# Four small edits to the loads and one to the layout at the head of a gated-linear-attention kernel

## The chip, the core and the metric

The kernel runs on one core of a Trainium2 chip. The metric is device microseconds from the start to the end of one execution. Times of several runs are compared by their median. Beside the timed runs there is one execution taken by the hardware profiler, from which all lines of the profile come.

## The reference

One residual layer with a gated linear attention mixer (GLA), then a squared-ReLU MLP, then a final RMSNorm, all in float32. There are 256 tokens, the model width is 2048, there are 4 heads with keys of 256 and values of 512, and chunks of 64 tokens. Cut to what matters:

```python
def _gla_mixer(h, w_in, w_gate_up, b_gate, o_norm, w_out):
    proj = h @ w_in                              # q, k, v, r, g_low (16 columns)
    log_a = log_sigmoid(g_low @ w_gate_up + b_gate) / 16.0
    cum = cumsum(log_a, within a chunk of 64);  total = cum at the chunk's end
    k_dec = k * exp(total - cum)
    # over the chunks: state = exp(total) * state + k_dec^T v;  o = (q / 16) @ state
    o = rmsnorm per head(o) * o_norm
    return (o * silu(r)) @ w_out

h = x + _gla_mixer(_rmsnorm(x, gla_norm), ...)
h = h + square(relu(_rmsnorm(h, mlp_norm) @ w_up)) @ w_down
out = _rmsnorm(h, final_norm)
```

## The kernel before

Each float32 matmul is made of three: an operand is split into a high part (`hi`, rounded to the matmul's own format, by ScalarE, L118) and the rest (`lo`, by VectorE, L131 or L165), and the products hi·hi, hi·lo and lo·hi are added up in PSUM. The weights come from memory once, in tiles of 128 rows (`raw`, six buffers), are split into `hi` and `lo` (five buffers each, of 1088 columns), and are used at once. `weights` does all this for one tile; SP's queue issues the loads, in order.

The work goes through stages. Only the first three matter here.

- **Stage 1** (`natural`, L176): 16 steps over `kt`, each with one tile of `w_vg` (the values' first 1024 columns and the 16 columns of the gate, 128 x 1040). A step is 24 matmuls: two halves of the tokens, three products, and the columns in four parts, of which three are 256 wide and one is 272. The stationary operand is the input, the moving one the weights. For the first two steps the tile is loaded and cast in pieces. The input itself, transposed (`xt`), is loaded in pieces of several `kt` each by `input_tile`, which is called while step `kt` is written; `x_loads` says at which step which piece is issued, and where it ends. `split_input` multiplies the input row by the norm's gain (`colt`, loaded from `cols`) and splits it (L326 on ScalarE, L327 on VectorE).
- **The key halves** (`turned`, L219): 8 pairs of `kt` for each of two halves of the key columns; a pair is one load of 2 x 128 rows by 512 columns and 24 matmuls, the first 12 with the pair's first 128 rows, the other 12 with its second. Here the weights are stationary and the input moves. The first half overlaps with the end of stage 1 and with the gate's own work (two transposes, L413, and eight matmuls, L422).
- **The query halves**, of the same form.

Behind these come the rest of the projections, the attention, the output projection (L715) and the MLP (L857), where GpSimd's queue issues loads that add into a tile in place (L734, L1067).

Small pieces of work are put between the steps by hand: `side` is a queue of functions, and `pump` calls one (or a few) after each step. `load_gate` in this queue issues the three loads of the gate's weights into `wgu`, and `split_gate` splits them into `wgs`. `tc.issue_after` orders an instruction behind another of the same engine; otherwise a scheduler with a cost model sets the order on each engine. [...]

Where operands lie within a tile is chosen by hand too. Input rows are 320 elements apart and are read by the key halves from element 64 on. A pair's weights lie from element 48 on, the second 128 rows directly behind the first, 512 elements further. With `gap` (the pairs listed in `even`), the second rows lie 16 elements further:

```python
between = SLOT - OFF - 2 * GT if gap else 0
to = [a[:, OFF - between : OFF + 2 * GT + between].rearrange("p (i c) -> p i c", i=2)[:, :, between:] for a in to]
```

so that they start at element 576, which, like 64, is a multiple of 32. The same is done at some later places of the kernel (`EVEN`, `BOTH`, `even` in `up`).

Of the kernel before, what the change touches and what calls it, by code (L numbers as in the profile page):

```python
# [36 lines left out]
KT = D // P  # L37
# [3 lines left out]
KEYW = HEADS * DK  # L41
RANK = 16
# [5 lines left out]
GT = 512  # L48
# [20 lines left out]
def tile_gla_mlp(ctx, tc, x, xt, cols, w_vg, w_in, w_gate, w_out, w_up, w_down, final_norm, out):  # L69
    nc = tc.nc  # L70
# [11 lines left out]
    def psum_bank(i, name="acc"):  # L82
        return psum.tile([P, 512], F32, tag=f"b{i}", name=name)

    def acc_banks(n):
        acc_free.rotate(-n)
        return [psum_bank(acc_free[k - n]) for k in range(n)]

    def aux_bank():
        aux_free.rotate(-1)  # L90
        return psum_bank(aux_free[-1], "aux")


    side = deque()

    def pump(n=1):

        with tc.issue_after(last_hi[0].ins), tc.issue_after(last_lo[0].ins):
            for _ in range(n):
                if side:  # L100
                    side.popleft()()
# [8 lines left out]
    last_load, last_hi, last_lo, last_sum, last_end = [None], [None], [None], [None], [None]  # L110

    def copy_hi(to, raw):
        with ExitStack() as order:
            if last_end[0]:
                order.enter_context(tc.issue_after(last_end[0]))
            if ordered[0]:
                order.enter_context(tc.issue_after(last_hi[0].ins))
            last_hi[0] = nc.scalar.copy(to, raw)  # L118

    def slots():  # L120
        return [wpool.tile([P, SLOT], F32R, tag=i, name=i) for i in ("hi", "lo")]

    def parts(raw, n, to, pieces=None):

        hi, lo = to
        for s in (slice(*p) for p in pieces or [(0, n)]):
            copy_hi(hi[:, s], raw[:, s])
            with ExitStack() as order:
                if last_sum[0]:
                    order.enter_context(tc.issue_after(last_sum[0]))  # L130
                last_lo[0] = nc.vector.tensor_tensor(lo[:, s], raw[:, s], hi[:, s].bitcast(F32), op=ALU.subtract)  # L131
        return hi, lo
# [3 lines left out]
    def raw_tile():  # L136

        if n_raw[0] is not None:
            n_raw[0] += 1
            if n_raw[0] % 7 == 0:  # L140
                return wpool.tile([P, G], F32, tag="more", name="raw", bufs=1)
        return wpool.tile([P, WMAX], F32, tag="raw", name="raw", bufs=6)

    def weights(src, n, pieces=None, room=None, gap=None):


        to = room or slots()
        raw = raw_tile()
        loads, pieces = pieces or ([(0, n)], [(0, n)])
        for s in (slice(*p) for p in loads):  # L150
            dst = raw[:, s]
            if len(src.shape) == 3:
                dst = dst.rearrange("p (i c) -> p i c", i=2)
                with ExitStack() as order:

                    if n_raw[0] == 7:
                        order.enter_context(tc.issue_after(last_load[0].ins))
                    last_load[0] = nc.sync.dma_start(out=dst, in_=src)
                between = SLOT - OFF - 2 * GT if gap else 0
                to = [a[:, OFF - between : OFF + 2 * GT + between].rearrange("p (i c) -> p i c", i=2)[:, :, between:] for a in to]  # L160
                copy_hi(to[0], dst)
                with ExitStack() as order:
                    if last_sum[0]:
                        order.enter_context(tc.issue_after(last_sum[0]))
                    last_lo[0] = nc.vector.tensor_tensor(to[1], dst, to[0].bitcast(F32), op=ALU.subtract)  # L165
                return to
            else:
                last_load[0] = nc.sync.dma_start(out=dst, in_=src[:, s])  # L168
        return parts(raw, n, to, pieces)

    def halves(o, x, w, first, last):
# [31 lines left out]
    def pair_of(w, kp, c0, even):  # L203
        return weights(w[2 * kp * P : 2 * (kp + 1) * P, c0 : c0 + GT].rearrange("(i p) c -> p i c", p=P), 2 * GT, gap=kp in even)

    def turned(row, w, c0, even=(0,), acc=None):

        acc = acc or acc_banks(GT // P // 2)
        for kp in range(KT // 2):
            wh, wl = pair_of(w, kp, c0, even)  # L210
            for i in range(2):
                kt = 2 * kp + i
                ah, al = row(kt)
                for j in range(GT // P):
                    s = slice(j * P, (j + 1) * P)
                    o = acc[j // 2][:, j % 2 * T : (j % 2 + 1) * T]
                    for n, (u, m) in enumerate(((wh, ah), (wh, al), (wl, ah))):

                        nc.tensor.matmul(  # L219
                            o, u[:, i, s], m, start=kt == 0 and n == 0 and j % 2 == 0,  # L220
                            stop=kt == KT - 1 and n == 2, skip_group_check=True,
                        )
                if kt < KT - 1:
                    pump()
        return acc
# [12 lines left out]


    colt = const.tile([P, 44], F32, name="colt")  # L240
    nc.scalar.dma_start(out=colt, in_=cols)
    g1 = lambda kt: colt[:, kt : kt + 1]
    g2 = lambda kt: colt[:, KT + kt : KT + kt + 1]
    go = lambda i: colt[:, 2 * KT + i : 2 * KT + i + 1]
# [28 lines left out]
    def x_row(kt, lo, hi):  # L273
        return [a[:, kt - CUT * (kt >= CUT), lo:hi] for a in xs[kt >= CUT]]

    stream_x = lambda kt: x_row(kt, WRAP, WRAP + T)
# [24 lines left out]
    xr = zz.rearrange("p a b t -> p (a b) t")  # L301
    cuts = [(0, 512), (512, 768), (768, WMAX)]
    x_done = [0]
    x_loads = {0: 1, 1: 3, 3: 6, 5: 9, 7: 12, 9: KT}

    def input_tile(kt):
        if kt in x_loads:
            s = slice(x_done[0], x_loads[kt])

            with ExitStack() as order:  # L310
                if kt >= 7:
                    order.enter_context(tc.issue_after(last_load[0].ins))
                nc.sync.dma_start(out=xr[:, s, :], in_=xv[:, s, :])
            x_done[0] = x_loads[kt]
        with ExitStack() as order:
            if kt >= FINE:
                order.enter_context(tc.issue_after(last_hi[0].ins))
                order.enter_context(tc.issue_after(last_lo[0].ins))
            split_input(kt)
        return ([(0, 512), (512, WMAX)], [(0, 256), (256, 512), (512, WMAX)]) if kt < 2 else None  # L320

    def split_input(kt):
        if kt == KT - 1:
            wrap_input(0, 0, CUT)
        h, l = x_row(kt, 0, T)
        nc.scalar.activation(h, xr[:, kt, :], AF.Copy, scale=g1(kt))  # L326
        nc.vector.scalar_tensor_tensor(l, xr[:, kt, :], g1(kt), h.bitcast(F32), op0=ALU.mult, op1=ALU.subtract)  # L327
        if kt in EVEN:
            i = EVEN.index(kt)
            nc.scalar.copy(xe[:, 0, i], h[:, :P].bitcast(F32))  # L330
            nc.vector.tensor_copy(xe[:, 1, i], l[:, :P].bitcast(F32))
# [3 lines left out]
    wgu = mid.tile([GR, KEYW], F32, tag="db", name="wgu")  # L335
# [8 lines left out]
    def load_h(t, half):  # L344
        c = slice(half * G, (half + 1) * G)
        with tc.issue_after(last_load[0].ins):
            nc.sync.dma_start(out=h[:, t, c], in_=x[t * P : (t + 1) * P, c])

    def load_gate():
        for p in (0, 32, 64):  # L350
            nc.scalar.dma_start(out=wgu[p : p + RANK, :], in_=w_gate)

    ms1 = st.tile([P, NT], F32, name="ms1")

# [17 lines left out]
        nc.vector.tensor_tensor(wgs[64:GR, :], wgu[64:GR, :], wgs[64:GR, :].bitcast(F32), op=ALU.subtract)  # L372

    nothing = lambda: None
    side.extend([clear_gate] + [nothing] * 4 + [load_gate] + [nothing] * 2 + [split_gate])
    side.extend([nothing, lambda: load_h(0, 0), lambda: load_h(0, 1), lambda: (load_h(1, 0), load_h(1, 1))])
    side.extend([lambda: token_ssq(0), lambda: (token_ssq(1), token_rsqrt())])


# [4 lines left out]
    def put_v(bank, n, t, c0):  # L384
# [4 lines left out]
        )  # L389

    acc = natural(plain_x, rows(w_vg, 0, WMAX), WMAX, cuts, ahead=input_tile)
    flush()
    wrap_input(1, 0, KT - CUT)
# [88 lines left out]
        nc.vector.tensor_tensor(kab[:, 0, c], kab[:, 0, c], zz[:, 1, c], op=ALU.mult)  # L482

    for half in range(2):
        acc = turned(stream_x, w_in, KEYW + half * GT, even=(0,) if half else (2, 3), acc=None if half else [aux_bank(), aux_bank()])
        for b in range(2):
            c0 = 4 * half + 2 * b
            from_bank(kab[:, 0, c0 : c0 + 2], acc[b])
# [15 lines left out]
    for half in range(2):  # L504
        acc = turned(stream_x, w_in, half * GT, even=())
# [41 lines left out]
    acc = natural(row_x, rows(w_in, 3 * KEYW), G, HALF, order=even_at(9, 11))  # L547
# [88 lines left out]
    acc = natural(lambda kt, t: (plain_x if kt == EVEN[1] else row_x)(kt, t), rows(w_in, 4 * KEYW), G, HALF, order=even_at(0, 6))  # L636
# [50 lines left out]
    acc = natural(row_x, rows(w_in, 5 * KEYW), G, HALF, order=even_at(2, 4))  # L687
# [322 lines left out]
    acc = [[], []]  # L1010
# [232 lines left out]
    for t in range(NT):  # L1243
# [19 lines left out]
        for on_act, lo, hi in ((0, 0, 256), (1, 1280, 1536), (0, 256, 768), (1, 1536, 2048), (0, 768, 1280)):  # L1263
            s = hf[:, t, lo:hi]
# [44 lines left out]
```

## Time and profile before

| | us |
|---|---|
| median of 3 runs | 1044.01 |
| lowest, highest | 1043.68, 1044.53 |
| the profiled execution, its time | 1044.42 |
| its span, from the first to the last instruction | 1042.4 |
| TensorE busy (matmuls) | 1034.2 |
| VectorE busy | 865.6 |
| ScalarE busy | 737.1 |
| GpSimd busy | 119.8 |

The granted TensorE clock was 0.998 of full speed over the span. Engines are named PE (TensorE matmul), PEld (its weight loads, which overlap), DVE (VectorE), ACT (ScalarE), POOL (GpSimd) and SP; a small q behind the name is the engine's queue, which issues loads. A row of the timeline gives the start, the duration, the engine, the line, the operation, output<-input, the shape, and in brackets the idle time of the engine ahead of it with what ended it. In groups of instructions x is the count, followed by busy time and the mean of one in ns. A row of the windows gives a stretch, its length, the busy time of an engine with its instructions, the granted clock, the share of DMA time and GB/s. In the chain of waits a row is start, duration, and what ran.

### The profile page before, as it was taken

Reading aid. Unit: us, or ns where it says so; the run is one execution under the profiler, and the core shown is the slowest. Engines: PE = TensorE matmul, PEld = TensorE weight load, DVE = VectorE, ACT = ScalarE, POOL = GpSimd, SP = SyncE. Lnnn points to the kernel's source line nnn. Section 1 sums busy time; section 2 is a strip of 40 time slices with the busy share of each in tenths; the row PEclk is TensorE's granted clock in tenths of the full one; section 3 lists DMA queues with packets and bytes.
Section 4 is the critical chain, followed back from the end, with each engine's and each line's share of the span. In section 5 each row is a group of like instructions: output and inputs, shape, how many; then the busy total and the mean of one; then the engine's idle time right before and its main releaser. Section 6 shows DMA issues by size and latency. Waiting matters only on the chain.

```text
span 1042.4 us, 23169 instructions
## 1 busy us (share of the span) xinstructions
PE 1034.2 (99%) x9058; PEld 1033.3 (99%) x9058; DVE 865.6 (83%) x1171; ACT 737.1 (71%) x1088; POOL 119.8 (11%) x163
## 2 busy tenths in 40 slices
PE   9999999999999999999999999999999999999997
PEld 9999999999999999999999999999999999999997
DVE  5768654656499876889999999999999999999887
ACT  6785544546477764677788788778778778878685
POOL 0000000010111101111111111111111111211100
PEclk9999999999999999999999999999999999999999
DMA  9957665555667786678887888887888888887772
GB/s 339 333 170 212 194 198 165 157 148 182 184 188 206 214 260 194 175 213 227 232 236 230 242 229 225 233 240 219 243 236 224 248 228 229 234 232 220 233 242 90
DMA packets 118733, 226.79 MB, mean 218 GB/s; under 512 B 10672, under 2 KB 27184, under 8 KB 118496
## 3 DMA queue, kind: packets, MB, share of 16 engines
q1 hardware_dynamic: 100096, 207.39, 63.3%
q0 software_dynamic: 17856, 16.26, 10.3%
q8 instruction: 71, 1.16, 0.4%
q10 hardware_dynamic: 672, 1.66, 0.4%
q14 instruction: 38, 0.31, 0.1%
HBM read 223.17 MB, written 2.10 MB: 216 GB/s over the span
## 4 chain that ended last, share of the span: by engine, by line
PE 96%; DMA 2%; issue 1%; ACT 0%; DVE 0%; SPq 0%; POOLq 0%; POOL 0%; DVEq 0%; ACTq 0%
PE up L857 33%; PE acc L857 28%; PE acc L176 17%; PE acc L715 8%; PE acc L219 6%; PE aux L219 2%; DMA raw<-in_w_vg 2%; PE aux L176 1%; PE aux L620 1%; PE aux L521 1%; DVE lo L131 0%; ACT hi L118 0%; ACT sqf L1196 0%; SPq L168 0%; PE acc L422 0%
## 5 line engine op out<-in xcount | busy, mean ns | idle before, releaser
L118 ACT CAST hi<-raw 128x512 fp32r<-128x512 f32 (+4 forms) x634 | 512.1, 834 | 231.5 <-PE acc L176 64.3
L131 DVE TENSOR_TENSOR lo<-raw,hi 128x768 fp32r<-128x768 f32 (+3 forms) x226 | 238.1, 1057 | 95.9 <-ACT hi L118 93.2
L857 PE MATMUL acc<-hi,act 128*128 128x256 f32 x1696 | 247.7, 276 | 0.0
L857 PE MATMUL up<-hh,hi 128*128 128x256 f32 x1024 | 238.7, 276 | 0.0
L857 PE MATMUL up<-hl,hi 128*128 128x256 f32 x1024 | 238.7, 276 | 0.0
L165 DVE TENSOR_TENSOR lo<-raw,hi 128x1024 fp32r<-128x1024 f32 x160 | 194.8, 1220 | 28.2 <-ACT hi L118 26.2
L857 PEld LDWEIGHTS acc<-hi,act 128*128 128x128 f32 x1696 | 217.6, 188 | 0.0
L857 PEld LDWEIGHTS up<-hh,hi 128*128 128x128 f32 x1024 | 192.3, 188 | 0.0
L857 PEld LDWEIGHTS up<-hl,hi 128*128 128x128 f32 x1024 | 192.3, 188 | 0.0
L1067 POOL DMA_DIRECT2D raw<-in_w_down x112 | 97.4, 869 | 516.9 <-DMA raw<-in_w_down 245.5
L1127 DVE TENSOR_TENSOR lo<-raw,hi 128x1024 fp32r<-128x1024 f32 x112 | 136.4, 1218 | 1.1 <-ACT hi L118 1.1
L857 PE MATMUL up<-hh,lo 128*128 128x256 f32 x1024 | 137.0, 276 | 0.0
L857 PE MATMUL acc<-lo,act 128*128 128x256 f32 x848 | 133.8, 276 | 0.0
L857 PEld LDWEIGHTS up<-hh,lo 128*128 128x128 f32 x1024 | 125.7, 188 | 0.0
L857 PEld LDWEIGHTS acc<-lo,act 128*128 128x128 f32 x848 | 113.3, 188 | 0.0
L176 PE MATMUL acc<-hi,xA 128*128 128x256 f32 (+1 forms) x728 | 105.2, 278 | 0.0
L176 PEld LDWEIGHTS acc<-hi,xA 128*128 128x128 f32 x728 | 93.5, 188 | 0.5 <-ACT hi L118 0.5
L598 DVE TENSOR_TENSOR raw<-raw 128x512 f32<-128x512 f32 x124 | 85.6, 691 | 3.2
L176 PE MATMUL acc<-lo,xA 128*128 128x256 f32 (+1 forms) x364 | 60.8, 278 | 0.1
L597 DVE TENSOR_TENSOR raw<-raw 128x256 f32<-128x256 f32 x124 | 52.4, 423 | 2.9
L176 PEld LDWEIGHTS acc<-lo,xA 128*128 128x128 f32 x364 | 50.3, 188 | 0.3 <-DVE lo L131 0.3
L219 PE MATMUL acc<-xA,hi 128*128 128x256 f32 x288 | 49.2, 276 | 0.0
(181 smaller groups left out, 1225.9 us busy)
## 6 DMA issues: line engine op xcount, KB each, us to landing
raw<-in_w_up SPq DMA_DIRECT2D x128, 512.0 KB, 4.5
raw<-in_w_down SPq DMA_DIRECT2D x224, 256.0 KB, 4.5
raw<-in_w_in SPq DMA_DIRECT2D x80, 512.0 KB, 3.7
raw<-in_w_down POOLq DMA_DIRECT2D x112, 128.0 KB, 5.2
raw<-in_w_out SPq DMA_DIRECT2D x20, 512.0 KB, 4.5
raw<-in_w_down SPq DMA_DIRECT2D x16, 512.0 KB, 4.9
raw<-in_w_vg SPq DMA_DIRECT2D x14, 520.0 KB, 8.4
raw<-in_w_out SPq DMA_DIRECT2D x24, 256.0 KB, 3.7
```

The source lines that it names most:

```text
L118: last_hi[0] = nc.scalar.copy(to, raw)
L131: last_lo[0] = nc.vector.tensor_tensor(lo[:, s], raw[:, s], hi[:, s].bitcast(F32), op=ALU.subtract)
L165: last_lo[0] = nc.vector.tensor_tensor(to[1], dst, to[0].bitcast(F32), op=ALU.subtract)
L176: nc.tensor.matmul(o[:, m], x, w[:, m], start=first and c == 0, stop=last, skip_group_check=True)
L219: nc.tensor.matmul(o, u[:, i, s], m, start=kt == 0 and n == 0 and j % 2 == 0, stop=kt == KT - 1 and n == 2, skip_group_check=True,)
L521: nc.tensor.matmul(o, kab[:, k[0], c0 + c, k[1] : k[1] + P], q(qt[:, c0 + c]), start=c == 0, stop=c == 1)
L597: nc.vector.tensor_tensor(u[:, 2], u[:, 0], u[:, 2], op=ALU.subtract)
L598: return nc.vector.tensor_tensor(u[:, 1::2], u[:, 1::2], u[:, 2:3].to_broadcast([P, 2, T]), op=ALU.subtract)
L715: newest[0] = nc.tensor.matmul(bank[:, o + d : o + d + T], x, w[:, d : d + T], start=bank in sums_banks and bank.name not in begun, stop=l ...
L857: newest[0] = nc.tensor.matmul(o, x, w, start=first, stop=last, skip_group_check=True).ins
L1067: nc.gpsimd.dma_start(out=raw[:, :T], in_=src[:, 0, T:], accum_op=ALU.add)
L1127: last_lo[0] = nc.vector.tensor_tensor(to[1][:, :G], u, to[0][:, :G].bitcast(F32), op=ALU.subtract)
```

## The change

- The three loads of the gate's weights are issued from GpSimd's queue and not from ScalarE's.
- The input comes in eight pieces and not in six; from the third on each ends earlier or is issued at a later step. The last two rows are issued at step 14 and no longer at step 9.
- The first piece of the first weight tile is issued from ScalarE's queue; the norms' columns, which ScalarE's queue had issued first, come from SP's queue, behind the first input piece.
- In the first key half, pair 0 joins pairs 2 and 3 in having its second rows 16 elements further.
- `split_gate` is called one step later in the side queue.

```diff
             else:
-                last_load[0] = nc.sync.dma_start(out=dst, in_=src[:, s])
+                queue = nc.sync if last_load[0] else nc.scalar
+                last_load[0] = queue.dma_start(out=dst, in_=src[:, s])
...
     colt = const.tile([P, 44], F32, name="colt")
-    nc.scalar.dma_start(out=colt, in_=cols)
...
-    x_loads = {0: 1, 1: 3, 3: 6, 5: 9, 7: 12, 9: KT}
+    x_loads = {0: 1, 1: 3, 3: 5, 5: 8, 8: 10, 10: 12, 12: 14, 14: KT}
...
                 nc.sync.dma_start(out=xr[:, s, :], in_=xv[:, s, :])
+            if kt == 0:
+                nc.sync.dma_start(out=colt, in_=cols)
...
         for p in (0, 32, 64):
-            nc.scalar.dma_start(out=wgu[p : p + RANK, :], in_=w_gate)
+            nc.gpsimd.dma_start(out=wgu[p : p + RANK, :], in_=w_gate)
...
-    side.extend([clear_gate] + [nothing] * 4 + [load_gate] + [nothing] * 2 + [split_gate])
-    side.extend([nothing, lambda: load_h(0, 0), lambda: load_h(0, 1), lambda: (load_h(1, 0), load_h(1, 1))])
+    side.extend([clear_gate] + [nothing] * 4 + [load_gate] + [nothing] * 3)
+    side.extend([split_gate, lambda: load_h(0, 0), lambda: load_h(0, 1), lambda: (load_h(1, 0), load_h(1, 1))])
...
     for half in range(2):
-        acc = turned(stream_x, w_in, KEYW + half * GT, even=(0,) if half else (2, 3), acc=None if half else [aux_bank(), aux_bank()])
+        acc = turned(stream_x, w_in, KEYW + half * GT, even=(0,) if half else (0, 2, 3), acc=None if half else [aux_bank(), aux_bank()])
```

In the order of instructions that follows, the identity and the zeroing on GpSimd are followed directly by the three gate loads. On ScalarE the two casts of the first weight piece now come ahead of the first input row, and on TensorE the first four matmuls are followed by four that need the second weight piece. The transposes of the gate stand after 59 and 62 matmuls of the first key half, where they stood after 67 and 70, and six of the gate's matmuls after 90, where they stood after 98. From the second key half on, TensorE's order is as before.

## The prediction

> **What bounds the kernel now.** I read the page first: how much of the span TensorE works.
>
> ```profile
> span 1042.4 us, 23169 instructions
> PE 1034.2 (99%) x9058; PEld 1033.3 (99%) x9058; DVE 865.6 (83%) x1171; ACT 737.1 (71%) x1088; POOL 119.8 (11%) x163
> ```
>
> TensorE is busy 1034.2 of 1042.4 us, so an edit can win only what TensorE waits, or what its matmuls take too long. Next, the view of who waited for whom, cut to TensorE's weight loads: after the warm-up these are all its waits in the whole span.
>
> ```profile
> PEld acc L176 <- ACT hi L118: 0.5, 2, 0.3
> PEld acc L176 <- DVE lo L131: 0.3, 1, 0.3
> ```
>
> All three belong to L176, and so to the first stage (16 steps over `w_vg`). Its steps begin where the timeline shows the first matmuls of a new `kt`; the view of busy time by stretches, one stretch per step (0, 1, 2, 3, 5, 6, 7; the first number after the stretch is its length), gives:
>
> ```profile
> 4.44:7.42 2.98, 2.98 (x25) 1.00 1.03 343
> 7.42:10.64 3.22, 3.22 (x27) 1.00 0.98 350
> 10.64:13.52 2.88, 2.88 (x27) 1.00 1.03 420
> 13.52:16.40 2.88, 2.88 (x27) 1.00 1.02 410
> 19.28:22.36 3.08, 3.04 (x26) 1.00 1.02 390
> 22.36:25.66 3.30, 3.25 (x24) 1.00 1.03 310
> 25.66:28.54 2.88, 2.88 (x26) 1.00 1.02 417
> ```
>
> An undisturbed step takes 2.88 us at a granted clock of 1.00. Steps 0 and 1 lose 0.10 and 0.34 us, steps 5 and 6 lose 0.20 and 0.42, the others shown nothing. So 0.44 us lies at the start and 0.62 us around 22 us. The second thing to be won is the spacing of matmuls of one and the same form (128x256). The chain of waits has long unbroken runs of them; the view of one line's instructions has their duration:
>
> ```profile
> 52.21 7.42 PE aux L219 x63
> 60.21 3.31 PE aux L219 x28
> 65.58 9.53 PE aux L219 x84
> L219 PE MATMUL aux<-xA,hi x32: 279/279/279, 52.8 to 58.3; 128*128 128x256 f32 x32
> L219 PE MATMUL acc<-xA,hi x7: 283/283/283, 76.4 to 77.5; 128*128 128x256 f32 x7
> L219 PE MATMUL acc<-xA,hi x271: 276/276/276, 77.9 to 134.6; 128*128 128x256 f32 x136
> ```
>
> 9.53 us / 84 is 113.5 ns a matmul; 7.42 / 63 is 117.8, and 3.31 / 28 is 118.2. So there is a quick pace (duration 276) and one 4.3 ns slower (279). The slow one holds from the first stage to about 63 us; the 283s at 76.4 to 77.5 are the second half of the pair that `even=(0,)` marks in the next half, and behind them the pace is quick. I read this as a lock: a disturbance throws TensorE into the slow pace, and a dozen matmuls whose weights lie at the same place as the input rows (weights at element 48+528=576, inputs at 64, both multiples of 32; an unmarked pair has its weights 16 off) put it back.
>
> **The change, part by part.**
>
> *Gate loads.* In the timeline, ScalarE's queue holds the three gate loads between two casts:
>
> ```profile
> 14.96 1.07 ACT L118 CAST hi<-raw 128x1040 fp32r<-128x1040 f32 x1 [0.41 <-DMA raw<-in_w_vg]
> 14.98 5.82 ACTq L351 DMA_DIRECT2D wgu<-in_w_gate  x3
> 20.84 0.51 ACT L326 ACTIVATE xA<-zz,colt 128x256 fp32r<-128x256 f32 x1 [4.82 <-DMA raw<-in_w_vg]
> 22.36 1.00 PEld L176 LDWEIGHTS acc<-hi,xA 128*128 128x128 f32 x8 [0.27 <-ACT hi L118]
> 23.64 0.41 PEld L176 LDWEIGHTS acc<-lo,xA 128*128 128x128 f32 x3 [0.27 <-DVE lo L131]
> ```
>
> The issues wait for earlier loads' semaphores, and behind them ScalarE, which has ended its cast at 16.03, stands still for 4.82 us. Step 6's input and weights are therefore late, and so is the second half of step 5. With the loads on GpSimd's queue nothing of ScalarE waits there: -0.62 us. What is next late: ScalarE then runs as far ahead as the five buffers of `hi` let it, a lead of over 2 us, so I expect nothing; the bounds are 0 and -0.62, and I take -0.62, since steps 2, 3 and 7, without such a hold, lose 0.00. The wait for the gate's landing falls on the cast into `wgs`, about 20 us later.
>
> On GpSimd the three issues stand behind the identity's last instruction:
>
> ```profile
> 2.08 0.29 POOL masks.py:199 TENSOR_SCALAR_AFFINE_SELECT ident<-ident 128x128 f32<-128x128 f32 x1
> L1067 POOL DMA_DIRECT2D raw<-in_w_down x112 | 97.4, 869 | 516.9 <-DMA raw<-in_w_down 245.5
> 42.72 1.07 POOL L356 TENSOR_TENSOR r<-ms,mhalf 128x1 f32<-128x1 f32 x2 [40.36 <-DVE ms L365]
> wgu<-in_w_gate ACTq DMA_DIRECT2D x3, 64.0 KB, 5.3
> 5.00:9.00 4.00, 4.00 (x33) 1.00 1.02 338
> 9.00:14.00 5.00, 5.00 (x44) 1.00 1.01 405
> ```
>
> They start at 2.4 us and take about 3 x 0.87 = 2.6 us of an idle engine; GpSimd's next work is at 42 us. But their 3 x 64 KB now move in the first microseconds, which are short of bytes: at the 338 GB/s of 5 to 9 us that is 0.58 us of transfer ahead of steps 1 and 2. It counts in the start, next.
>
> *First weights on ScalarE's queue, columns on SP's.*
>
> ```profile
> 0.73 0.42 ACTq L241 DMA_DIRECT2D colt<-in_cols  x1
> 1.17 0.89 SPq L168 DMA_DIRECT2D raw<-in_w_vg  x2
> 3.16 0.51 ACT L326 ACTIVATE xA<-zz,colt 128x256 fp32r<-128x256 f32 x1 [0.49 <-DMA colt<-in_cols]
> 3.90 0.71 ACT L118 CAST hi<-raw 128x256 fp32r<-128x256 f32 x2 [0.23 <-DMA raw<-in_w_vg]
> 4.44 1.21 PE L176 MATMUL acc<-hi,xA 128*128 128x256 f32 x8
> 4.91 0.63 ACT L118 CAST hi<-raw 128x528 fp32r<-128x528 f32 x1 [0.29 <-DMA raw<-in_w_vg]
> 8.37 0.53 PEld L176 LDWEIGHTS acc<-hi,xA 128*128 128x128 f32 x4 [0.20 <-ACT hi L118]
> 9.01 1.06 ACT L118 CAST hi<-raw 128x1040 fp32r<-128x1040 f32 x1 [0.69 <-DMA raw<-in_w_vg]
> ```
>
> The first 256 KB took 3.90 - 1.17 = 2.73 us from issue to use; issued at 0.73 they are there at 3.46 (3.90 at worst, if the transfer and not the issue sets it). The columns took 3.16 - 0.73 = 2.43; from 1.17 they come at 3.60. ScalarE now casts both pieces first and scales the input row third: casts 3.46 to 4.17, input 4.17 to 4.68 (5.12 at worst). So the first matmul comes at 4.70 and not at 4.44. In the changed order TensorE does four matmuls and then stands before the second piece's cast, which ends at 5.54 as now (4.68 + 0.63 = 5.31 if that piece comes earlier too, 5.75 if the input ends at 5.12). Twenty matmuls of about 0.12 us follow: step 0 ends near 7.98 (7.75 to 8.20), now 7.42. Step 1 loses its 0.34 us, because what it waited for at 8.37 is wanted only nine matmuls after 7.98, at 9.04: a margin of 0.67 that covers the 0.58 of gate bytes. Step 2 then begins at 7.98 + 2.88 = 10.86, now 10.64. Its cast, 10.07 + 0.58 at worst, is covered too. The start costs +0.2 us (0.0 to +0.5).
>
> [...]
>
> *Input pieces.* Six loads become eight, two more issues of about 0.4 us each on SP's queue, which waits often in this stretch; a piece is now issued just ahead of its own step's weights, five to six weight buffers ahead of TensorE. The DMA issues of the first 60 us show the larger pieces' flight:
>
> ```profile
> zz<-in_xt SPq DMA_DIRECT2D x3, 384.0 KB, 7.9
> zz<-in_xt SPq DMA_DIRECT2D x1, 512.0 KB, 11.9
> ```
>
> Cover: that lead, some 5 x 2.88 = 14.4 us, against flights of 7.9 to 11.9 us. Cost 0; without the lead, a wait at steps 10, 12 and 14, as at step 6 now (0.3 each).
>
> *The pair.* Pair 0 of the first key half gets the offset. Its second half runs at the 283 pace (12 x about 2 ns: +0.02). Then the quick pace should hold over pair 1 and the first half of pair 2, up to the two transposes of the gate: 35 x 4.3 ns = -0.15. In the changed order these stand after 59 and 62 of the half's matmuls (before: 67 and 70), so that pair 2's marked half comes nearly whole behind them and can restore the pace a half pair earlier: 12 x 4.3 = -0.05. Sum -0.18; bounds +0.02 (no effect) and -0.18.
>
> [...]
>
> **Sum.** +0.20 - 0.62 - 0.18 = -0.60 us. The profiled execution (span 1042.4, time 1044.42) would become a span of 1041.8 and 1043.82. It stood 0.41 above the median of the three runs (1044.01; they span 1043.68 to 1044.53), so the median becomes 1043.4. That is 0.06%: real, but far below 0.2% (2.1 us), about what a measurement of this kernel can tell from no change.
>
> **The rivals.**
> - *The start loses more.* The gate's bytes and the columns hold the first weights up by 1.2 us and not 0.58: step 1's cast ends at 9.57 against 9.04, step 2's lower part comes later in turn, and the start costs some 0.95. It decides once the start costs over 0.80. For it: 338 GB/s against 405 later. Against: the margin of 0.67. Time 1044.2. Chance 0.12.
> - [...] Chance 0.12. [...]
> - *The stall moves.* The late pieces hold steps 10 to 14: two waits of 0.3 give 1044.0. Chance 0.10.
> - *Slower.* GpSimd's queue also carries the 112 accumulating loads of L1067. If three more software loads ahead shift their slots so that one comes late, TensorE stops in the up and down stages and falls into the slow pace, where now
>
> ```profile
> L857 PE MATMUL acc<-hi,act 128*128 128x256 f32 x1696 | 247.7, 276 | 0.0
> ```
>
>   all run at 276. Two thousand matmuls at 4.3 ns more are 8.6 us: 1052.6. It decides at the first stop of TensorE there. Against: the order of instructions is the same from the second key half on, and GpSimd is idle 516.9 us ahead of these loads. Chance 0.03.
> - *Faster.* The first stage itself falls into the quick pace: 384 x 4.3 ns = 1.65 us more, 1041.8. Nothing in it lies at the same place. Chance 0.03.
>
> **How the numbers follow.** The forecast has the remaining 0.60. Range: the cases at 1043.4, 1043.6, 1044.0 and 1044.2, the start's 0.0 to +0.5, and the runs' own spread of 0.4 either way give 1042.6 to 1044.5. Faster by over 0.2% (below 1041.9) only in the last rival, 0.03; slower by over 0.2% in the rival before it and a little for what I don't see, 0.04; within 0.2%, 0.93.
>
> **What would show it.** Steps 5 and 6 of 2.88 us, and no wait of ScalarE for a weight load of 4.82 us; the first matmul near 4.7, step 2 near 10.9; in the first key half 276s from pair 1 on; the three gate loads on GpSimd before 5 us. Wrong: a wait of TensorE past 24 us, step 2 after 11.4, or 279s throughout the first key half.

## The result: 1.8 us slower, outside the range

| | before | after |
|---|---|---|
| median | 1044.16 (15 runs, 1043.68 to 1045.17) | 1045.95 (15 runs, 1045.60 to 1047.12) |
| ratio, with its 95% interval | | 1.0017 (1.0010 to 1.0025) |
| the profiled execution, its time | 1044.42 | 1045.80 |

The forecast was 1043.4 us, with a range from 1042.6 to 1044.5. The median stays within 0.2% of before, as was thought likeliest, but on the other side, and 1.45 us above the range. The two profiled executions differ by 1.38 us. Of the experiments' runs further down one, of the kernel with pair 5 marked, took 1299.74 us at a granted clock of 0.753; the median given for that kernel is that of its nine other runs.

The page of the kernel after, its first lines:

```profile
span 1043.8 us, 23179 instructions
PE 1035.3 (99%) x9058; PEld 1034.7 (99%) x9058; DVE 865.7 (83%) x1171; ACT 737.0 (71%) x1088; POOL 121.3 (12%) x166
```

The span grew by 1.4 us, and TensorE's busy time by 1.1 with the same 9058 matmuls: most of the loss is not seen as idle time but as matmuls that took longer. The waits of TensorE's weight loads agree. Of the three of before none is left; behind the warm-up there is one, at the first matmul:

```profile
PEld acc L177 <- ACT xA L328: 0.6, 1, 0.6
```

The stretches of the kernel after: the first eight matmuls, then the steps 0, 1, 2, 5 and 6 of the first stage (length, TensorE's busy time and matmuls, granted clock, DMA share, GB/s):

```profile
5.13:7.03 1.90, 1.90 (x8) 1.00 0.99 316
5.13:8.97 3.84, 3.84 (x25) 1.00 1.01 319
8.97:11.97 3.00, 3.00 (x27) 1.00 1.03 403
11.97:15.00 3.03, 3.03 (x27) 1.00 1.03 418
20.76:23.64 2.88, 2.88 (x27) 1.00 1.03 417
23.64:26.52 2.88, 2.88 (x27) 1.00 1.03 418
```

Steps 5 and 6 take 2.88 us each, as forecast, and lose nothing any more. But step 1 begins at 8.97 instead of 7.42, step 3 at 15.00 instead of 13.52, and step 7 at 26.52 instead of 25.66. The first stage is worth +0.86 us where -0.42 was forecast.

The timeline of the kernel after, around the first matmuls, and ahead of it one row of the kernel before for the first cast of step 1's weights:

```profile
6.87 1.45 ACT L118 CAST hi<-raw 128x256 fp32r<-128x256 f32 x3
```
```profile
2.33 1.66 POOL L353 DMA_DIRECT2D wgu<-in_w_gate  x3
3.96 0.71 ACT L118 CAST hi<-raw 128x256 fp32r<-128x256 f32 x2 [1.28 <-DMA raw<-in_w_vg]
4.58 0.50 ACT L328 ACTIVATE xA<-zz,colt 128x256 fp32r<-128x256 f32 x1
8.45 1.32 ACT L118 CAST hi<-raw 128x256 fp32r<-128x256 f32 x3 [0.37 <-DMA raw<-in_w_vg]
```

The gate's loads are issued where expected. The first weights are cast at 3.96, no sooner than the 3.90 of before, and the input row comes behind them, so the first matmul starts at 5.13. Step 1's first weights are cast at 8.45 and not at 6.87: they wait for their load.

The first key half, by the chain of waits (start, length, what ran) and by the duration of one group of its matmuls:

```profile
52.95 6.62 PE aux L220 x56
...
63.43 0.71 PE acc L424 x6
...
66.50 9.90 PE aux L220 x84
```
```profile
L220 PE MATMUL aux<-xE,hi x32: 279/279/279, 70.6 to 76.0; 128*128 128x256 f32 x32
```

The last 84 matmuls of the half take 9.90 us and not 9.53: 117.9 ns each, where they were 113.5. Before, the quick pace held from about 63 us on. Now it is there for the twelve matmuls of pair 3's first half, ahead of the gate's six (L424), and gone again behind them, as eight of the matmuls on either side show:

```profile
L220 PE MATMUL aux<-xA,hi x8: 276/276/276, 61.2 to 62.3; 128*128 128x256 f32 x8
L220 PE MATMUL aux<-xA,hi x8: 276/279/279, 64.7 to 65.9; 128*128 128x256 f32 x8
```

From the start of step 7 to the end of these 84 it is 66.50 + 9.90 - 26.52 = 49.88 us; before it was 65.58 + 9.53 - 25.66 = 49.45. That is +0.43 where -0.18 was forecast. The two together make +1.29 of the span's +1.4; behind the first key half nothing of size was added.

### The profile page after: what moved, and what is told of

It is laid out like the page before. It is cut to its first block, busy times and chain, and to the rows that moved or that the text cites. A ratio compares the mean times of both kernels' runs of the same rounds, so it can differ in the third digit from the quotient of the medians.

```text
span 1043.8 us, 23179 instructions
## 1 busy us (share of the span) xinstructions
PE 1035.3 (99%) x9058; PEld 1034.7 (99%) x9058; DVE 865.7 (83%) x1171; ACT 737.0 (71%) x1088; POOL 121.3 (12%) x166
## 4 chain that ended last, share of the span: by engine, by line
PE 98%; issue 0%; DMA 0%; ACT 0%; DVE 0%; POOLq 0%; POOL 0%; DVEq 0%
PE up L859 33%; PE acc L859 28%; PE acc L177 19%; PE acc L717 8%; PE acc L220 6%; PE aux L220 2%; PE aux L177 1%; PE aux L622 1%; PE aux L523 1%; DMA raw<-in_w_vg 0%; ACT sqf L1198 0%; PE acc L424 0%; DVE hf L1270 0%; ACT hi L118 0%; POOLq L1307 0%
```

## The experiments

The theory after this result has three parts. The gate's loads, through GpSimd's queue in the first microseconds, make the first weights late. The swap of the first loads delays the first matmul and wins nothing. The gate's matmuls, which the changed order puts 8 places earlier in the first key half, undo the quick pace. The rival for the first part is that bytes alone are to blame and not the queue; for the third, that the mark on pair 0 itself does harm. A fourth question came up with the results: what the 0.62 us of ScalarE's hold are worth in other executions. The expectations of the first runs held another theory (A in the first two): that the late first matmul leaves TensorE at half its pace (213 ns from one matmul to the next instead of 118), and that the gate's loads do no harm. The first run contradicted it.

In the table the start of step 7 stands for all that the first stage has lost, and the time from there to the end of the last 84 matmuls for the pace of the first key half, both from one profiled execution (the view of stretches and the chain, worked out as above). The last column is the median less that of the runs of before on the same chip; the intervals of the single ratios are about 0.001 (1 us) either way. The four parts alone ran on one chip; the kernels with late gate loads, with the gate's loads back on ScalarE, and with pair 5 marked on a second; the remaining experiments on a third.

| kernel | step 7 starts | from there to the end of the 84 | first of the gate's six stands behind matmul | less before, us |
|---|---|---|---|---|
| before | 25.66 | 49.45 | 98 | |
| before, again | 25.55 | 49.45 | 98 | -0.20 (one run) |
| pair 0 marked alone | 25.96 | 49.32 | 98 | -0.08 |
| late gate loads, pair 0 | 25.61 | 49.31 | 98 | +0.06 |
| input pieces alone | 25.64 | 49.86 | 92 | +0.69 |
| first loads alone | 25.95 | 49.90 | 96 | +0.78 |
| after, gate loads on ScalarE | 25.95 | 49.89 | 90 | +0.61 |
| after, gate loads late on GpSimd | 25.91 | 49.89 | 90 | +0.85 |
| gate loads early on ScalarE | 26.27 | 49.86 | 90 | +0.85 |
| after | 26.52 | 49.88 | 90 | +1.79 |
| after, again | 26.63 | 49.88 | 90 | +1.73 (one run) |
| after, pair 5 marked too | 26.58 | 49.69 | 90 | +0.93 (nine runs) |
| gate loads alone | 26.98 | 49.90 | 96 | +1.70 |
| after, longer warm-up | 27.19 | 49.88 | 90 | +2.23 (one run) |

**The parts of the change alone.** Four kernels, each the one before with one edit.

*Gate loads alone.*

```diff
-            nc.scalar.dma_start(out=wgu[p : p + RANK, :], in_=w_gate)
+            nc.gpsimd.dma_start(out=wgu[p : p + RANK, :], in_=w_gate)
```

> The kernel before, with only the three gate loads moved to GpSimd's queue. Theory A (the loss is a late first matmul that leaves TensorE at half pace, and comes from the order of the first loads and casts, not from the gate): first matmul near 4.44 as before, full pace from there, steps 5 and 6 at 2.88 us, so 0.4 to 0.6 us faster than before. Rival B (the gate's 192 KB in the first microseconds make the start late): steps 0 and 1 lose 0.5 us or more against before, which eats the 0.62 won at steps 5 and 6, so the time is as before or up to 0.5 us longer. In both the gate's matmuls stand after 96 of the first key half, outside the marked half pair, so that the quick pace holds from there.

Measured: 1046.05 us, ratio 1.0017 (1.0007 to 1.0026). This edit alone costs about as much as the whole change, more than either expectation allowed. Its waits, steps 0 and 1, and the cast of the second piece of the first weights:

```profile
PEld acc L176 <- ACT hi L118: 1.6, 2, 0.9
```
```profile
4.49:9.38 4.89, 3.74 (x24) 1.00 0.95 279
9.38:12.53 3.15, 3.15 (x24) 1.00 1.03 403
```
```profile
6.54 0.63 ACT L118 CAST hi<-raw 128x528 fp32r<-128x528 f32 x1 [1.83 <-DMA raw<-in_w_vg]
```

Before, that cast ran at 4.91, behind 0.29 us of waiting; here TensorE stands still twice in step 0, for 1.6 us in all, and the step takes 4.89 us at 279 GB/s where it took 2.98 at 343. A further 0.45 us of the 1.70 lie in the key half (49.90 for 49.45): with the gate's six matmuls behind 96 the quick pace did not hold, against what both theories expected.

*First loads alone*: the first weight piece by ScalarE's queue, the columns by SP's.

```diff
-                last_load[0] = nc.sync.dma_start(out=dst, in_=src[:, s])
+                queue = nc.sync if last_load[0] else nc.scalar
+                last_load[0] = queue.dma_start(out=dst, in_=src[:, s])
...
-    nc.scalar.dma_start(out=colt, in_=cols)
...
+            if kt == 0:
+                nc.sync.dma_start(out=colt, in_=cols)
```

> The kernel before, with only the first weights on ScalarE's queue and the columns on SP's. Theory A: the first matmul comes at about 5.0 instead of 4.44, the matmuls from there to about 7 us are 213 ns apart instead of 118, and the third step begins 1 us or more later than 10.64; the time is 0.7 to 1.3 us longer. Rival B: without the gate's bytes the first weights are there early enough, the pace is 118 ns from the first matmul, step 2 begins within 0.3 us of 10.64, and the time is within 0.3 us of before.

Measured: 1045.13 us, ratio 1.0007 (0.9998 to 1.0016). The timeline has the issue of the first weights, their cast, the warm-up and the first matmuls:

```profile
0.74 0.42 ACTq L169 DMA_DIRECT2D raw<-in_w_vg  x1
3.99 0.71 ACT L118 CAST hi<-raw 128x256 fp32r<-128x256 f32 x2 [1.31 <-DMA raw<-in_w_vg]
1.06 3.48 PE L252 MATMUL aux<-ones 128*128 128x128 f32 x16 [1.06 <-DVE ones L249]
5.16 1.03 PE L177 MATMUL acc<-hi,xA 128*128 128x256 f32 x6 [0.62 <-ACT xA L328]
```

Issued 0.43 us sooner (0.74 for 1.17), the first weights were cast 0.09 us later than before, and the first matmul came at 5.16. Theory A had the time about right, but not the cause: the first six matmuls took 1.03 us, so hardly any of the slow pace is left here, and 0.45 of the 0.78 us lie in the key half (49.90). Step 7 starts 0.3 to 0.4 us later than in the two executions of before, but no later than with pair 0 alone (25.96), which leaves the start as it was. So the swap wins nothing; what it costs at the end of the stage is not told apart from the spread of one start.

*Input pieces alone.*

```diff
-    x_loads = {0: 1, 1: 3, 3: 6, 5: 9, 7: 12, 9: KT}
+    x_loads = {0: 1, 1: 3, 3: 5, 5: 8, 8: 10, 10: 12, 12: 14, 14: KT}
```

> The kernel before, with only the input in eight later pieces. The gate's six matmuls now stand after 92 of the first key half, inside pair 3's marked half. Theory L (matmuls of another kind inside a marked half undo the quick pace): durations of 279 ns stay from there to the next marked half near 77 us, some 100 matmuls at 4.3 ns, so 0.4 to 0.5 us longer than before. Rival M (the position does not matter): 276 ns from pair 4 on, and the time within 0.1 us of before.

Measured: 1045.04 us, ratio 1.0008 (0.9999 to 1.0017). Step 7 starts at 25.64, and the list of TensorE's waits holds none of the first stage, so no piece is late; but the same group of matmuls in the first key half now has the slow duration:

```profile
L219 PE MATMUL aux<-xE,hi x32: 279/279/279, 69.7 to 75.1; 128*128 128x256 f32 x32
```

An edit that only moves loads of the first stage costs 0.41 us in the key half: it moved the gate's six matmuls from 98 to 92, and the two transposes from 67 and 70 to 60 and 64.

*Pair 0 alone.*

```diff
-even=(0,) if half else (2, 3)
+even=(0,) if half else (0, 2, 3)
```

> The kernel before, with only pair 0 of the first key half marked. The gate's matmuls stand where they stood (after 67, 70, 98, 108). Theory P (as predicted): 276 ns over pair 1 and the first half of pair 2, 0.15 us shorter than before. Rival Q (the marked half does not take, as in the changed kernel's trace): 279 ns up to the gate's matmuls, the time unchanged within 0.05 us. The start is that of the kernel before, so this run also shows whether the start repeats: first matmul at 4.44, full pace from the third matmul on.

Measured: 1044.27 us, ratio 0.9999 (0.9990 to 1.0009). Its chain:

```profile
52.51 7.29 PE aux L219 x63
...
65.75 9.53 PE aux L219 x84
```

The run of 63 takes 7.29 us where it took 7.42, and the last 84 keep their quick 9.53. The mark does what was forecast of it as long as the gate's matmuls stay at 98: 0.13 us, too little for the runs to show. It does no harm by itself, and as input pieces alone lose the pace without that mark, the rival of the third part falls.

**The gate's loads within the whole change.** Two kernels, the one after with the gate's loads elsewhere: back on ScalarE's queue, and on GpSimd's queue but behind an instruction that reads step 5's input row.

```diff
-            nc.gpsimd.dma_start(out=wgu[p : p + RANK, :], in_=w_gate)
+            nc.scalar.dma_start(out=wgu[p : p + RANK, :], in_=w_gate)
```

> The changed kernel with the gate loads back on ScalarE's queue, all else changed. Theory A (the gate's bytes in the first microseconds are the largest part of the loss): step 7 of the first stage begins within 0.3 us of the run with the first weights alone (25.95), the key half still loses 0.47 us because the gate's matmuls stand after 90, and the time is 0.8 to 1.2 us below the changed kernel, near 1045.0. Rival B (the order of the first loads and casts is the largest part): the time stays within 0.4 us of the changed kernel.

```diff
+        held = const.tile([P, 1], F32, name="held")
+        row = x_row(5, 0, 1)[0].bitcast(F32)
+        hold = nc.gpsimd.tensor_tensor(held, row, mhalf, op=ALU.mult)
-        for p in (0, 32, 64):
-            nc.gpsimd.dma_start(out=wgu[p : p + RANK, :], in_=w_gate)
+        with tc.issue_after(hold.ins):
+            for p in (0, 32, 64):
+                nc.gpsimd.dma_start(out=wgu[p : p + RANK, :], in_=w_gate)
```

> The changed kernel, with the gate loads on GpSimd's queue held until the input row of step 5 is split (a multiplication of one column of that row on GpSimd stands ahead of them), so about 14 us later. Theory A (the time at which these bytes move matters, not the queue): as in the run with the gate on ScalarE's queue or up to 0.3 us better, near 1044.9. Rival C (loads built by software cost, whenever they are issued): no better than 0.4 us below the changed kernel.

Measured: 1045.02 us, ratio 1.0006 (0.9997 to 1.0016), and 1045.26 us, ratio 1.0008 (0.9998 to 1.0018). Against the +1.79 of the kernel after 0.9 to 1.2 us are gone, by the start of step 7 only 0.6. The kernel with pair 5 marked, which ran on the same chip and starts its step 7 like the kernel after (26.58), stands at +0.93 with 0.20 us less in the key half; against it the two win 0.5 and 0.3 us. The rest of the larger difference stays open. The first, with step 1's cast, and steps 0 and 1; then the second's loads and its step 1:

```profile
7.06 1.47 ACT L118 CAST hi<-raw 128x256 fp32r<-128x256 f32 x3
```
```profile
5.17:8.68 3.51, 3.51 (x24) 1.00 0.99 355
8.68:11.55 2.87, 2.87 (x26) 1.00 0.97 372
```
```profile
16.27 1.69 POOL L357 DMA_DIRECT2D wgu<-in_w_gate  x3
```
```profile
8.64:11.52 2.88, 2.88 (x27) 1.00 0.97 363
```

Without the gate's bytes the same cast runs at 7.06 and not at 8.45, and step 1 loses nothing. Step 7 starts at 25.95 and 25.91, against 26.52. So loads at 16 us on GpSimd's queue do no harm here, and the same loads at 2.33 us do. The two differ in one thing more: the first still has ScalarE's hold and the second has not, and yet their steps 7 start 0.04 us apart. The hold was worth nothing here.

**The queue or the bytes.** The kernel before, with the gate's loads on ScalarE's queue as there, but issued in the first microseconds:

```diff
-    side.extend([clear_gate] + [nothing] * 4 + [load_gate] + [nothing] * 2 + [split_gate])
+    side.extend([nothing] * 8 + [split_gate])
...
+    clear_gate()
+    load_gate()
```

> The kernel before, with the three gate loads left on ScalarE's queue but issued at the start, behind the columns (near 2.7 to 3.7 us), where GpSimd's queue issued them at 2.3 to 4.0. Theory A1 (their bytes at that time are what costs): the weights' pieces of steps 0 and 1 land as late as with GpSimd's queue, step 7 near 26.9, and the time 1.2 us or more above before. Rival A2 (loads built by software in that time cost more than their bytes): step 7 near 26.0, and, with the key half's loss (the gate's matmuls stand after 90), the time 0.3 to 0.7 us above before.

Measured: 1045.13 us, ratio 1.0009 (0.9999 to 1.0019). Steps 0 and 1, and the cast of the second piece:

```profile
4.49:8.81 4.32, 4.05 (x24) 1.00 1.01 313
8.81:11.87 3.06, 3.06 (x26) 1.00 1.02 413
```
```profile
6.32 0.63 ACT L118 CAST hi<-raw 128x528 fp32r<-128x528 f32 x1 [1.72 <-DMA raw<-in_w_vg]
```
```profile
6.05 0.33 SPq L313 DMA_DIRECT2D zz<-in_xt  x1
```

Step 7 and the time lie between what the two theories expected. The bytes are the same, and the second piece is about as late as through GpSimd's queue (6.32 against 6.54), but what follows recovers sooner: step 0 takes 4.32 us and not 4.89, and step 7 starts at 26.27 and not at 26.98. The five traces whose first loads are those of before, without early gate bytes, start step 7 at 25.55 to 25.96. Against these the early bytes cost 0.3 to 0.7 us, and the same bytes through GpSimd's queue 1.0 to 1.4. So, by an estimate from these starts, the bytes explain about a third to a half of that loss. The medians, each less its own before, stand 0.85 us apart (+0.85 and +1.70), about as the starts of step 7 do (0.71). That all of this rest is the queue is not shown, since the two kernels differ in more: on ScalarE's queue the gate's loads are issued from 1.89 us on and not from 2.33, and SP's next load of the input comes at 6.05 us (the row above), where it came at 4.01 before and at 4.03 with GpSimd's queue. If that delay counts, the bytes' share is smaller still.

**The pace of the first key half.** The kernel after, with pair 5 marked too, which lies behind all of the gate's matmuls:

```diff
-even=(0,) if half else (0, 2, 3)
+even=(0,) if half else (0, 2, 3, 5)
```

> The changed kernel with pair 5 of the first key half marked too, behind the last of the gate's matmuls. Theory L (the gate's matmuls inside pair 3's marked half undo the quick pace, and the next marked half behind them restores it): 279 ns up to pair 5, 283 in its second half, 276 from pair 6 on; some 60 matmuls at 4.3 ns, so 0.25 us below the changed kernel. Rival M (something else keeps the slow pace in this half): 279 ns to its end, no change. Step lengths of the first stage as in the changed kernel, so this run shows as well how far its start repeats.

Measured: 1045.34 us, 0.6 us below the median of the kernel after, of which the key half shows 0.19. Its chain and its group of matmuls:

```profile
66.57 9.70 PE aux L220 x84
```
```profile
L220 PE MATMUL aux<-xE,hi x32: 276/276/276, 70.7 to 75.9; 128*128 128x256 f32 x32
```

From pair 6 on all matmuls are quick, and the half wins 0.19 us back. So the pace that was missing can be had by a mark with none of the gate's matmuls behind it. The counts show where these stand: 24 matmuls make a pair, so pair 3's second half is the matmuls from 84 to 95. At 90 or 92 the six lie within it, at 96 directly behind it; at 98, two matmuls later, the pace survived in all four traces that have them there, and in the ten others it was lost (in one of them up to pair 5's mark). In the eight of these with the six at 90 or 92, pair 3's first half is quick, as in the kernel after above: pair 2's mark had taken, and the loss comes with the six. The transposes are not the cause: in the trace with the longer warm-up they stand after 47 and 59, ahead of pair 2's marked half, and the pace comes and goes just the same. Why two matmuls are enough, the runs do not tell. That pair 0's mark, which wins 0.13 with the gate at 98, wins nothing in the changed order (6.62 / 56 = 118.2 ns) stays open too.

**What the hold is worth.** The kernel before with both: the gate's loads late on GpSimd (as above), and pair 0 marked, so that ScalarE's hold is gone and the gate's matmuls stay at 98.

> The kernel before, with only the gate loads on GpSimd's queue, held until step 5's input row as in the run above, and pair 0 marked. The gate's matmuls stand after 67, 70, 98 and 108 as before. Theory A: the start is that of the kernel before, no wait of ScalarE near 16 us, steps 5 and 6 at 2.88 us, the key half 0.13 us shorter, so 0.2 to 0.75 us faster than before (the less, the later the first step ends, because a late TensorE hides ScalarE's stop). Rival C (software loads cost whenever they come): no faster than before.

Measured: 1044.47 us, ratio 1.0001 (0.9991 to 1.0010). By the prediction's terms it should have won 0.62 + 0.13, and theory A expected 0.2 to 0.75; it won nothing that the runs show. Rival C had the time, but not the cause, as the rows show no harm from the loads. The step at 22.73 lasts 2.88 us, and the first run of the key half 7.29:

```profile
22.73:25.61 2.88, 2.88 (x27) 1.00 1.02 335
```
```profile
52.16 7.29 PE aux L219 x63
```

Both effects are there, and still step 7 starts at 25.61, only 0.05 us ahead of the kernel before. A second execution of each of the case's two kernels says why.

> The kernel before once more, for a second look at its start. [...] Rival F (the start of the kernel before is fixed): first matmul 4.44, no 213 ns spacing, step 3 at 13.5, step 7 at 25.66 within 0.1.

Measured: 1044.08 us. The first nine matmuls, steps 0, 5 and 6, and ScalarE around the gate's loads in this second execution of the kernel before:

```profile
4.49:6.34 1.85, 1.85 (x9) 1.00 1.01 302
4.49:8.27 3.78, 3.78 (x24) 1.00 0.99 330
19.79:22.66 2.87, 2.87 (x26) 1.00 1.00 363
22.66:25.55 2.89, 2.89 (x27) 1.00 1.04 294
```
```profile
15.84 4.50 ACTq L351 DMA_DIRECT2D wgu<-in_w_gate  x3
20.39 0.51 ACT L326 ACTIVATE xA<-zz,colt 128x256 fp32r<-128x256 f32 x1 [3.51 <-DMA raw<-in_w_vg]
```

ScalarE stands still for 3.51 us here too, and steps 5 and 6 lose nothing. TensorE is already later by then, because its first nine matmuls took 1.85 us, about 206 ns each; in the execution from which the forecast was made, ten took 1.21:

```profile
4.44:5.65 1.21, 1.21 (x10) 1.00 1.05 329
```

The granted clock stands at 1.00 in both rows. So the 0.62 us of the hold and the 0.8 us of a slow first step are not two losses that add up: whichever comes, the other is mostly hidden, and step 7 starts at 25.55 or at 25.66. Four undisturbed steps, 3 to 6, are 11.52 us. The six traces with the hold took, from step 3 to step 7, 12.14 us in the first execution of before (13.52 to 25.66), and little or nothing more than 11.52 in the other five: 11.52 in the second execution of before (14.03 to 25.55), 11.60 with pair 0 alone (14.36 to 25.96), 11.52 with the input pieces alone (14.12 to 25.64) and with the first loads alone (14.43 to 25.95), and 11.51 in the kernel after with the gate's loads on ScalarE (14.44 to 25.95).

> The changed kernel once more. [...] Rival F: half pace to 7.03 and step 7 at 26.52 within 0.1, because the pause ahead of the first matmul sets it.

Measured: 1046.01 us. In the second execution of the kernel after the first matmuls are quick, and step 0 takes the same 3.84 us, now with TensorE idle:

```profile
5.16:9.00 3.84, 3.23 (x25) 1.00 1.04 322
```
```profile
PEld acc L177 <- ACT hi L118: 0.8, 1, 0.8
```

Step 1 starts at 8.97 or 9.00, whatever the pace, since its weights are not there earlier: their first cast starts at 8.45 and 8.54, after ScalarE has waited 0.37 and 0.39 us for their load. In the first execution the slow pace had hidden that wait.

**The slow first matmuls.** The kernel after with 14 rounds of warm-up matmuls and not 8:

```diff
-WARM = 8
+WARM = 14
```

> The changed kernel with 14 warm-up products instead of 8 (28 matmuls of 213 ns, so no pause of TensorE until 7 us if the pace stays). [...] Rival F (the pause causes the half pace): the warm-up's spacing falls near 4.5 us, where the kernel before reached its full pace.

Measured: 1046.51 us. Its warm-up (from the second matmul on) and step 0:

```profile
1.43:6.76 5.33, 5.33 (x26) 1.00 0.90 258
```
```profile
6.98:9.91 2.93, 2.93 (x25) 1.00 1.03 322
```

The starts of the second and the twenty-seventh warm-up matmul lie 5.33 us apart, so 213 ns for each of 25 steps; the matmuls of the first stage behind them are quick (2.93 us for step 0). Rival F falls: TensorE has no pause here, and the spacing of 213 ns stays past 4.5 us, up to 6.76. The slow pace ended neither at one time nor behind one number of matmuls: within the warm-up with the first loads alone (its sixteen matmuls took 3.48 us, where they took 3.63 before), about the first matmul, at 4.44 us, in the first execution of before, behind some nine more, at 6.34, in the second, behind eight more, near 7 us, in the first of after (eight matmuls up to 7.03, 238 ns each on average), and here not before the twenty-seventh matmul of the warm-up. As two executions of the same kernel differ in it, the program alone does not set it; what does, no run here shows. The longer warm-up won nothing: the first stage's matmuls begin at 6.98, and step 7 at 27.19. The column of the granted clock shows none of it: it stands at 1.00 over the slow matmuls too.

## Why the prediction was wrong

- *Gate loads, start.* The step that failed is the sentence on the margin: step 1's late weights were to be wanted "only nine matmuls after 7.98", and 0.67 us were to cover the 0.58 us of gate bytes. The 0.58 was worked out as bytes at 338 GB/s. Measured: step 1's first cast moved by 1.58 us (6.87 to 8.45) in the changed kernel, 1.39 of it by the gate's loads (7.06 without them). So not the ninth matmul of step 1 but the first waited for its weights, and step 1 began at 8.97 and not at 7.98. Step 7 started 0.6 us later for the gate's loads; the medians give 0.3 to 0.5 us on one chip, and 0.9 to 1.2 against the kernel after. The rival "The start loses more" had the mechanism and the 1.2 us, and was given 0.12; its own price of 0.95 for the start was too low as well (1.33 by the start of step 2).
- *First weights on ScalarE's queue.* The 3.46 us for their arrival failed: 3.96 in the changed kernel. The sum took issue as what sets the arrival. The traces speak against it: issued 0.43 us sooner, the weights were cast at 3.99 with the swap alone, where they were cast at 3.90 before. The prediction's worst case, 3.90, in which the transfer and not the issue sets it, came nearer. So the first matmul came 0.43 us later than the forecast 4.70, and 0.7 later than before. At step 7 the swap alone stands at 25.95, inside the 25.55 to 25.96 of the traces without it.
- *ScalarE's hold.* The reading of the rows was right: the wait of 4.82 us is gone and steps 5 and 6 take 2.88. But in the second execution of before these steps take 2.87 and 2.89 too, with the hold in place, so the sign did not show the cause. The step that failed is taking the -0.62 as the end of the bounds that counts. It was subtracted from an execution whose start happened to be quick; in the five other traces with the hold, whose step 3 starts 0.5 to 0.9 us later, it cost 0.08 us or nothing. The other bound, 0, was the better one.
- *The pair.* Its mechanism was right where the order of before stands: 0.13 us, as forecast for that part (0.15 less 0.02). In the changed order pair 0's mark did not take. That pair 2's mark would restore the pace a half pair earlier came as forecast (276 at 61.2 to 62.3 us). The step that failed is that the sum priced the move of the two transposes alone and put the move of the gate's six matmuls, from 98 to 90, at nothing. At 90 these lie in pair 3's marked half, and behind them the pace is lost up to the half's end: +0.43 and not -0.18. The range counted a case at 1043.6, in which the pair is worth nothing, whether by itself or through the gate's matmuls. No run shows it: pair 0 alone won its 0.13 us in this half, and in the whole change the half lost not the gain only, but 0.43 us of the pace that the kernel before already had.
- *Input pieces.* Cost 0 was right for the loads: no wait of TensorE past the first step. But by the scheduler's order the edit alone moved the gate's matmuls and cost 0.41.
- *GpSimd's accumulating loads, the first stage's quick pace.* Neither rival came: 1.29 us of the span's 1.4 are there at the end of the first key half.

By the forecast's own terms the first stage was missed by 1.28 us (+0.86 for -0.42) and the key half by 0.61 (+0.43 for -0.18). The profiled executions moved by 1.38; the medians by 1.79, of which the rest is that the execution of before lay 0.26 above its median and that of after 0.15 below.

No kernel here beats the one before by more than the runs tell: the pair alone stands at 0.9999 (0.9990 to 1.0009).

## What to carry to other kernels

A stall seen in one execution is worth its length only if nothing else makes the same engine late ahead of it: here the hold that cost 0.62 us in one execution cost 0.08 or nothing in five others. Look at a second execution before subtracting. Keep loads that nothing needs soon out of the first microseconds, however idle their queue is: the gate's 192 KB there made step 7 start 0.3 to 0.7 us later on ScalarE's queue, and 1.0 to 1.4 on GpSimd's. When an edit moves instructions on TensorE, price every one that moves, and also the effects that the old order protected: here four small edits of the loads each shifted the same six matmuls, and that shift cost 0.41 to 0.45 us each time.

## What the runs showed that was not expected

- The same 192 KB, issued in the first microseconds of the kernel before, made step 7 start 0.3 to 0.7 us later through ScalarE's queue and 1.0 to 1.4 us through GpSimd's.
- At a granted clock of 1.00 the matmuls started 213 ns apart for some 3 to 6 us from the first warm-up matmul on (at 1.05 us); those of the first stage were then about 120 ns apart. The end of the slow pace moved between executions from ahead of 4.5 us to nearly 7. In the two executions of the kernel after, where it differed, step 1 started at 8.97 and 9.00 all the same, since it waits for its weights.
- The quick pace of 113.5 ns, once set by a marked pair, survived six other matmuls two places behind the marked half (four traces), and not six that stand directly behind it or within it (ten traces).
